# Down projection of a conv-FFN by seven quadrant products with operand sums made by accumulating DMAs in DRAM

## Chip, cores and metric

The kernel runs on one core of a Trainium2 chip. The metric is device time in microseconds (us) of one execution. TensorE, VectorE (DVE), ScalarE (ACT), GpSimd (POOL) and SyncE (SP) run side by side and wait for one another by semaphores; the last two and ScalarE also issue DMAs, which run on 16 DMA engines.

## The reference, cut to what matters

A decoder layer: a mixture of three token mixers, an output projection, and a gated FFN with a causal depthwise convolution of three taps. Sequence 1024, width 1024, FFN width 2816. The change touches the last three lines.

```python
def reference(x, norm_mix_g, w_in, ..., norm_ffn_g, w_up, conv_f_w, w_down, rel_bias, final_g):
    ...
    x = x + y @ w_out[l]
    h = rmsnorm(x, norm_ffn_g[l])
    up = causal_dwconv(h @ w_up[l], conv_f_w[l])
    gate, val = jnp.split(up, 2, axis=-1)
    x = x + (jax.nn.silu(gate) * val) @ w_down[l]
    return rmsnorm(x, final_g)
```

## The kernel before, in words

All data are float32. A product is made of three TensorE passes (`mm3`, L89 to 92): each operand is split into a rounded part `hi` and the rest `lo` (`split`, L69: a copy on ScalarE, a subtraction on VectorE or GpSimd), and hi·hi, hi·lo and lo·hi are added up in PSUM. A matmul has a 128x128 stationary and a 128x512 moving tile.

**Up projection.** `main(j)` (L973), j = 0 to 21, makes feature tile j of the gate and of the value half for 1024 tokens. It already uses seven products of quadrants instead of eight: GpSimd makes four sums of weight quadrants (L981 to 984), each operand is split into one of six slots, and TensorE runs five products of 12 matmuls (`t2`, `t3`, `t1`, `t4`, `b22`) and two more (`b11`, `b21`) for a feature tile four further on (`lead`, L945): 84 matmuls, 60 in mains 6, 13, 20 and 21, which have no lead. The weights of a main come by two DMAs on SP (L975, L976) into one of two pairs of buffers (`ur`, `xp`), the lead's by a third (L942). At the end of a main ScalarE and VectorE do the convolution (`conv3`, L967), ScalarE the SiLU (L1015), VectorE the multiplication by the value (L1016), and SP stores the 128x1024 activation tile to DRAM (`actd`, L1017). GpSimd issues no DMA in this part.

**Down projection.** For each half h of the tokens (L1079) all 22 feature tiles are run through. For tile kt, `wd_tiles` (L1045) loads 128x1024 of `w_down` and 128x512 of `actd`, splits both, and TensorE adds into eight PSUM banks (four token blocks of 128 by two halves of the output columns): 24 matmuls a tile. The operands of the first two tiles are loaded and split ahead, in the places of `b11` and `b21` (`early_tiles`, L955). The eighth bank runs behind, and for the last three tiles (`LAG`) the order is by bank, so that banks end one after the other. Then VectorE adds the residual (L1108, loaded back from `x2d`), ScalarE sums squares (L1110), and `finish` (L1061) scales by the final norm and stores the output.

The order of TensorE's work is the order in the source; that of the other engines is planned at build time from modelled durations, with `tc.issue_after` forcing some of it. Each engine, SP's and GpSimd's DMA queue too, then runs its list in order: an instruction that waits for a semaphore holds up those behind it.

## Time and profile before

| | us |
|---|---|
| median of 3 runs | 1180.95 (1178.72 to 1181.68) |
| the profiled execution | 1175.46 |
| its span, first to last instruction | 1173.7 |
| TensorE busy | 1132.8 (97%) |
| VectorE busy | 757.5 (65%) |
| GpSimd busy | 523.5 (45%) |
| ScalarE busy | 503.7 (43%) |

The profiled execution lies 5.5 us below the median of the runs. "Busy" counts overlapping matmuls once; the rate of matmuls is read from their starts. The up projection's mains run from about 525 to 924 us of the span, the down projection from 924 us to the end. A row of a timeline gives start and duration in us, the engine, the line of the kernel, the operation, what it writes and reads, and in brackets the idle time before it and what ended it.

### The profile page before, as it was taken

To read this page: it belongs to the slowest core of one execution; us is meant where nothing else is said; L and a number is where in the kernel's file an instruction comes from. 1 tells how busy PE (TensorE), PEld (TensorE's weight loads), DVE (VectorE), ACT (ScalarE), POOL (GpSimd) and SP (SyncE) were. 2 spreads that over 40 slices of the span, in tenths; PEclk is the share of its full clock that TensorE was granted. 3 is DMA by queue.
4 is the path that set the end of the run, shared out by engine and by line. 5 is a ranking of instruction groups with operands and counts; after the bars stand their busy time and mean duration, and the time that the engine had idled before them with its cause. 6 is when DMAs were issued, how large, how long until landed. Compare 5 with 4: busy or idle time off the path is not lost.

```text
span 1173.7 us, 14302 instructions
## 1 busy us (share of the span) xinstructions
PE 1132.8 (97%) x5327; PEld 939.6 (80%) x5327; DVE 757.5 (65%) x886; ACT 503.7 (43%) x802; POOL 523.5 (45%) x332
## 2 busy tenths in 40 slices
PE   9999979999989999889999999999999999999997
PEld 7888867788878888778887888888887788888886
DVE  7599965456676667794768877688778722164214
ACT  7212105255566564653444444444445432333323
POOL 4223533333333112036867877777876042334331
PEclk9999989999999999989999999999999999999999
DMA  6217312977797514313333342332423564456531
GB/s 240 72 54 222 86 54 81 261 215 168 174 323 160 111 30 151 139 53 114 95 121 95 108 139 90 126 108 91 142 91 125 170 206 156 140 184 214 180 113 72
DMA packets 58741, 160.70 MB, mean 137 GB/s; under 512 B 6168, under 2 KB 15888, under 8 KB 58672
## 3 DMA queue, kind: packets, MB, share of 16 engines
q1 hardware_dynamic: 45360, 141.37, 36.9%
q0 software_dynamic: 12160, 16.78, 7.6%
q10 hardware_dynamic: 1152, 1.64, 0.5%
q8 instruction: 42, 0.69, 0.2%
q14 instruction: 27, 0.22, 0.1%
HBM read 124.02 MB, written 32.60 MB: 133 GB/s over the span
## 4 chain that ended last, share of the span: by engine, by line
PE 86%; DVE 5%; DMA 4%; ACT 3%; issue 2%; POOL 1%; ACTq 0%; DVEq 0%; POOLq 0%; SPq 0%
PE cb L90 8%; PE cb L91 8%; PE cb L92 8%; PE d_ps L92 7%; PE d_ps L91 6%; PE d_ps L90 6%; PE ca L92 4%; PE ca L90 4%; PE ca L91 4%; PE pv_ps L585 2%; PE f_ps L90 2%; PE f_ps L92 2%; PE f_ps L91 2%; PE t_ps L554 2%; DMA w_raw<-in 1%
## 5 line engine op out<-in xcount | busy, mean ns | idle before, releaser
L72 POOL TENSOR_TENSOR w_lo<-w_raw,w_hi 128x512 fp32r<-128x512 f32 (+2 forms) x51 | 107.9, 2121 | 180.1 <-ACT w_hi L71 180.1
L970 DVE SCALAR_TENSOR_TENSOR x<-ut,pr,x 128x1024 f32<-128x1024 f32 x88 | 149.9, 1720 | 19.1 <-ACT x L968 18.3
L72 POOL TENSOR_TENSOR wd_lo<-w_raw,wd_hi 128x1024 fp32r<-128x1024 f32 x32 | 78.4, 2455 | 161.7 <-ACT wd_hi L71 149.1
L92 PE MATMUL d_ps<-wd_hi,a_lo 128*128 128x512 f32 x336 | 130.8, 389 | 1.2 <-DVE a_lo L72 1.2
L90 PE MATMUL d_ps<-wd_hi,a_hi 128*128 128x512 f32 x336 | 130.8, 389 | 0.5 <-ACT a_hi L71 0.5
L91 PE MATMUL d_ps<-wd_lo,a_hi 128*128 128x512 f32 x336 | 130.8, 389 | 0.5 <-POOL wd_lo L72 0.5
L72 DVE TENSOR_TENSOR a_lo<-a_raw,a_hi 128x512 fp32r<-128x512 f32 x42 | 41.8, 1004 | 126.7 <-ACT a_hi L71 120.7
L71 ACT CAST w_hi<-w_raw 128x512 fp32r<-128x512 f32 (+2 forms) x63 | 46.3, 747 | 134.4 <-PE v L92 23.6
L298 DVE SCALAR_TENSOR_TENSOR yc<-u,pr,yc 128x1024 f32<-128x1024 f32 x60 | 89.6, 1546 | 1.7 <-ACT yc L295 1.4
L92 PEld LDWEIGHTS d_ps<-wd_hi,a_lo 128*128 128x128 f32 x336 | 63.1, 188 | 14.4 <-DVE a_lo L72 1.5
L90 PEld LDWEIGHTS d_ps<-wd_hi,a_hi 128*128 128x128 f32 x336 | 63.1, 188 | 14.1 <-ACT a_hi L71 1.0
L91 PEld LDWEIGHTS d_ps<-wd_lo,a_hi 128*128 128x128 f32 x336 | 63.1, 188 | 14.0 <-POOL wd_lo L72 0.8
L71 ACT CAST a_hi<-a_raw 128x512 fp32r<-128x512 f32 x42 | 25.8, 621 | 107.2 <-PE d_ps L91 104.7
L968 ACT ACTIVATE x<-ut,pr 128x1024 f32<-128x1024 f32 x44 | 50.8, 1154 | 42.7 <-DVE ut L1010 29.2
L541 ACT ACTIVATE p<-p,mn 128x128 f32<-128x128 f32 (+3 forms) x64 | 49.7, 777 | 32.7 <-DVE mn L538 32.5
L71 ACT CAST wd_hi<-w_raw 128x1024 fp32r<-128x1024 f32 x42 | 43.9, 1047 | 23.3 <-DMA w_raw<-in 23.3
L1007 DVE TENSOR_TENSOR ut<-cb,yb 128x512 f32<-128x512 f32 x22 | 15.2, 690 | 57.1 <-PE cb L92 57.1
L565 DVE TENSOR_TENSOR ptl<-t_ps,pth 128x512 fp32r<-128x512 f32 x48 | 33.1, 689 | 22.7 <-ACT pth L564 22.2
L1016 DVE TENSOR_TENSOR x<-x 128x1024 f32<-128x1024 f32 x22 | 40.7, 1848 | 10.6 <-ACT x L1015 10.6
L554 PE MATMUL t_ps<-ident,p 128*128 128x128 f32 x288 | 44.7, 272 | 1.5 <-ACT p L541 1.1
L981 POOL TENSOR_TENSOR xp<-xp 128x512 f32<-128x512 f32 x11 | 20.0, 1819 | 55.1 <-DVE so_lo L72 43.7
L554 PEld LDWEIGHTS t_ps<-ident,p 128*128 128x128 f32 x288 | 35.7, 140 | 10.3 <-ACT p L541 1.5
(409 smaller groups left out, 3312.6 us busy)
## 6 DMA issues: line engine op xcount, KB each, us to landing
w_raw<-in SPq DMA_DIRECT2D x93, 512.0 KB, 3.7
xp<-in SPq DMA_DIRECT2D x26, 512.0 KB, 3.8
ur<-in SPq DMA_DIRECT2D x22, 512.0 KB, 3.5
actd<-x SPq DMA_DIRECT2D x22, 512.0 KB, 5.5
a_raw<-actd SPq DMA_DIRECT2D x42, 256.0 KB, 3.1
vd<-vt SPq DMA_DIRECT2D x8, 512.0 KB, 3.3
vv<-vd POOLq DMA_DIRECT2D x8, 512.0 KB, 5.4
g<-fs SPq DMA_DIRECT2D x8, 512.0 KB, 5.8
```

Of the source, the lines that this page charges most:

```text
L71: cp = A.copy(hi, src)
L72: lo_eng.tensor_tensor(out=lo, in0=src, in1=f(hi), op=ALU.subtract)
L90: T.matmul(ps, whi, xhi, start=start, stop=False, **kw)
L91: T.matmul(ps, whi, xlo, start=False, stop=False, **kw)
L92: T.matmul(ps, wlo, xhi, start=False, stop=stop, **kw)
L298: V.scalar_tensor_tensor(out=yc[i], in0=u[i][:, j:j + S], scalar=col("cwc", j * 2 + i), in1=yc[i], op0=ALU.mult, op1=ALU.add)
L541: mark["exp"] = A.activation(out=p[:, :n], in_=p[:, :n], func=AF.Exp, scale=-1.0, bias=mn[:, ix:ix + 1], accum_out=den[h // 2][:, dc:dc + 1])
L554: T.transpose(out=tp[:, i * P:(i + 1) * P], in_=p[:, kj * P:(kj + 1) * P], identity=ident)
L565: mark["v"] = V.tensor_tensor(out=tl[:, o:o + n], in0=tp[:, :n], in1=f(th[:, o:o + n]), op=ALU.subtract)
L968: A.activation(out=c, in_=t[:, 2:], func=AF.Copy, scale=col("cwf", 2 * 44 + m))
L970: V.scalar_tensor_tensor(out=c, in0=t[:, q:q + S], scalar=col("cwf", q * 44 + m), in1=c, op0=ALU.mult, op1=ALU.add)
L1016: V.tensor_tensor(out=cg, in0=cg, in1=cv, op=ALU.mult)
```

## The change

The down projection is written as a product of 2x2 quadrants and done by seven products P1 to P7 instead of eight. Quadrants of the activations: first or second 11 feature tiles (`HF`) by first or second 512 tokens. Quadrants of `w_down`: the same feature halves by output-column halves. The tiles of the second feature half are stored with the opposite sign (an operation of VectorE with scalar -1.0 in place of the multiplication), so that the differences that the scheme needs become sums.

The products want four sums of weight quadrants (T1 to T4) and four of activation quadrants (`s12` in both halves, `s3d`, `s4d`). All are made in DRAM while the up projection runs: for weights, SP copies a quadrant from DRAM to DRAM (`t_copy`, four chunks of three or two tiles per sum, mains 2 to 9) and GpSimd issues a DMA that adds another quadrant, or an earlier sum, into it (`t_add`, mains 4 to 12). The activation tile is stored two or three times (`store`), and GpSimd issues DMAs that add into the stored tiles (`sums`), up to three per main; the last ones come in steps 1, 4 and 8 of the down projection. The stores of the last two mains go out on ScalarE's queue.

In the down projection each product takes 11 steps. In a step `down_tiles` loads two 128x512 tiles (five buffers each), both are split by ScalarE and VectorE (none by GpSimd), and TensorE runs 12 matmuls into four banks; the products use two groups of four banks in turn, and P3 adds to the banks of P5. The order is P1, P2, P6, P7, P5, P4, P3. Four tiles instead of two are prepared ahead. At a product's end its four banks are combined with the residual tiles (`done1` to `done7`); the second half of the tokens is finished after P4, the first after P3.

```diff
-    actd = [dr.tile([P, S], F32, name=f"actd{j}") for j in range(FT)]
...
+    HF = FT // 2
+    CH = ((0, 3), (3, 6), (6, 9), (9, 11))
+    tsum = {n: [dr.tile([P, b - a, 544], F32, name=f"T{n}_{c}")[:, :, :512] for c, (a, b) in enumerate(CH)] for n in (1, 2, 3, 4)}
+    s12 = [dr.tile([P, S], F32, name=f"s12_{i}") for i in range(HF)]
+    s3d, s4d, a1d = ([dr.tile([P, 512], F32, name=f"{n}_{i}") for i in range(HF)] for n in ("s3d", "s4d", "a1d"))
+    a2d = [dr.tile([P, S], F32, name=f"a2d_{i}") for i in range(HF)]
+    def wquad(half, q, a, b):
+        return w_down[(half * HF + a) * P:(half * HF + b) * P, HS[q]]
+    def rows(x):
+        return x.rearrange("(t p) c -> p t c", p=P)
+    def t_copy(n, c):
+        half, q = {1: (0, 0), 3: (0, 1), 2: (1, 1), 4: (1, 0)}[n]
+        nc.sync.dma_start(out=tsum[n][c], in_=rows(wquad(half, q, *CH[c])))
+    def t_add(n, c):
+        src = rows(wquad(*{1: (0, 1), 3: (1, 1)}[n], *CH[c])) if n in (1, 3) else tsum[n // 2][c]
+        G.dma_start(out=tsum[n][c], in_=src, accum_op=ALU.add)
+    TCOPY = [(n, c) for c in range(4) for n in (1, 3, 2, 4)]
+    TADD = ((1, 0), (3, 0), (1, 1), (2, 0), (3, 1), (4, 0), (1, 2), (2, 1), (3, 2), (4, 1), (1, 3), (2, 2),
+            (3, 3), (4, 2), (2, 3), None, (4, 3), None)
+    def t_sums(j):
+        if j >= 2:
+            with tc.issue_after(mark["wu"].ins):
+                for x in TCOPY[2 * (j - 2):2 * (j - 1)]:
+                    t_copy(*x)
+    def sums(j):
+        if j >= 4:
+            with tc.issue_after(mark["a12"].ins):
+                for x in TADD[2 * (j - 4):2 * (j - 3)]:
+                    if x:
+                        t_add(*x)
+        i = j - 1
+        if 0 <= i < HF:
+            G.dma_start(out=s3d[i], in_=s12[i][:, HS[1]], accum_op=ALU.add)
+        for back, dst, src in ((1, lambda i: s12[i][:, HS[1]], lambda i: a2d[i][:, HS[1]]),
+                               (2, lambda i: s12[i][:, HS[0]], lambda i: s12[i][:, HS[1]]),
+                               (3, lambda i: s4d[i], lambda i: s12[i][:, HS[0]])):
+            i = j - back - HF
+            if 0 <= i < HF:
+                G.dma_start(out=dst(i), in_=src(i), accum_op=ALU.add)
+    def store(j, cg):
+        i = j % HF
+        if j < HF:
+            dst = ((s12[i], cg), (a1d[i], cg[:, HS[0]]), (s3d[i], cg[:, HS[0]]))
+        else:
+            dst = ((a2d[i], cg), (s4d[i], cg[:, HS[0]]))
+        for o, x in dst:
+            (nc.scalar if j >= FT - 2 else nc.sync).dma_start(out=o, in_=x)
+    def a_of(t, q=None):
+        return lambda i: t[i] if q is None else t[i][:, HS[q]]
+    def b_of(half, q):
+        return lambda i: wquad(half, q, i, i + 1)
+    def t_of(n):
+        return lambda i: tsum[n][i // 3][:, i % 3, :]
+    SRC = {"P1": (a_of(a1d), b_of(0, 0)), "P2": (a_of(a2d, 0), b_of(1, 0)), "P6": (a_of(s12, 0), t_of(2)),
+           "P7": (a_of(s3d), t_of(3)), "P5": (a_of(s12, 1), t_of(1)), "P4": (a_of(a2d, 1), t_of(4)),
+           "P3": (a_of(s4d), b_of(1, 1))}
...
-        b = bop[("b11", "b21")[kt]]
+        hi, lo = bop[("b11", "b21")[kt // 2]]
         raw = wp.tile([P, D], F32, name="w_raw", tag="w_raw", bufs=2)
-        nc.sync.dma_start(out=raw, in_=w_down[kt * P:(kt + 1) * P, :])
-        hi, lo = (t.rearrange("p k c -> p (k c)") for t in b)
-        split(raw, hi[:, :1024], lo[:, :1024], V)
-        ar = f(hi[:, 1536:])
-        nc.sync.dma_start(out=ar, in_=actd[kt][:, HS[0]])
-        split(ar, hi[:, 1024:1536], lo[:, 1024:1536], V)
-        return hi[:, :1024], lo[:, :1024], hi[:, 1024:1536], lo[:, 1024:1536]
+        r = []
+        for n, src in enumerate(SRC["P1"]):
+            x = raw[:, HS[n]]
+            nc.sync.dma_start(out=x, in_=src(kt))
+            k = 2 * (kt % 2) + n
+            split(x, hi[:, k, :], lo[:, k, :], V)
+            r += [hi[:, k, :], lo[:, k, :]]
+        return r
...
-        nc.sync.dma_start(out=g, in_=w_up[2 * j])
+        mark["wu"] = nc.sync.dma_start(out=g, in_=w_up[2 * j])
+        t_sums(j)
...
+            mark["a12"] = G.tensor_tensor(out=a12, in0=a12, in1=a11, op=ALU.subtract)
...
         o = operand(a12, G)
+        sums(j)
...
-        V.tensor_tensor(out=cg, in0=cg, in1=cv, op=ALU.mult)
-        nc.sync.dma_start(out=actd[j], in_=cg)
+        if j < HF:
+            V.tensor_tensor(out=cg, in0=cg, in1=cv, op=ALU.mult)
+        else:
+            V.scalar_tensor_tensor(out=cg, in0=cg, scalar=-1.0, in1=cv, op0=ALU.mult, op1=ALU.mult)
+        store(j, cg)
...
-            early[j - FT + 3] = early_tiles(j - FT + 3)
-    close(c_um, c_h2, held["xp"], c_y, c_mm)
+            for q in range(2):
+                early[2 * (j - FT + 3) + q] = early_tiles(2 * (j - FT + 3) + q)
...
+    NBUF = LAG + 2
+    x3 = [dn.tile([P, D], F32, name=f"x3_{t}") for t in range(8)]
+    for e in "ab":
+        for n, dt in (("raw", F32), ("hi", F32R), ("lo", F32R)):
+            for _ in range(NBUF):
+                dn.tile([P, 512], dt, name=f"{e}_{n}", tag=f"{e}_{n}", bufs=NBUF)
+    p1, u2, u3 = ([dn.tile([P, 512], F32, name=f"{n}_{t}") for t in range(4)] for n in ("p1", "u2", "u3"))
...
-    def wd_tiles(kt, h):
-        if h == 0 and kt in early:
-            return early[kt]
-        hs = slice(h * 512, (h + 1) * 512)
-        raw = wp.tile([P, D], F32, name="w_raw", tag="w_raw", bufs=2)
-        nc.sync.dma_start(out=raw, in_=w_down[kt * P:(kt + 1) * P, :])
-        wh = dn.tile([P, D], F32R, name="wd_hi", tag="wd_hi", bufs=NBUF)
-        wl = dn.tile([P, D], F32R, name="wd_lo", tag="wd_lo", bufs=NBUF)
-        split(raw, wh, wl, V if kt % 4 == 3 else G)
-        ar = dn.tile([P, 512], F32, name="a_raw", tag="a_raw", bufs=NBUF)
-        nc.sync.dma_start(out=ar, in_=actd[kt][:, hs])
-        ah = dn.tile([P, 512], F32R, name="a_hi", tag="a_hi", bufs=NBUF)
-        al = dn.tile([P, 512], F32R, name="a_lo", tag="a_lo", bufs=NBUF)
-        split(ar, ah, al, V)
-        return wh, wl, ah, al
+    def down_tiles(n, kt):
+        r = []
+        for e, src in zip("ab", SRC[n]):
+            raw = dn.tile([P, 512], F32, name=f"{e}_raw", tag=f"{e}_raw", bufs=NBUF)
+            mark["down"] = nc.sync.dma_start(out=raw, in_=src(kt))
+            hi = dn.tile([P, 512], F32R, name=f"{e}_hi", tag=f"{e}_hi", bufs=NBUF)
+            lo = dn.tile([P, 512], F32R, name=f"{e}_lo", tag=f"{e}_lo", bufs=NBUF)
+            split(raw, hi, lo, V)
+            r += [hi, lo]
+        return r
+    def square(t, dh):
+        q = HS[dh]
+        A.activation(out=xo[t % 2][:, q], in_=x3[t][:, q], func=AF.Square,
+                     accum_out=s3[:, 2 * t + dh:2 * t + dh + 1])
...
+            (nc.scalar if last is not None and q == HS[0] else nc.sync if t < 4 else G).dma_start(
+                out=out[t * P:(t + 1) * P, q], in_=x[:, q])
...
+    def dmm(n, y, t, kt, ops, start=True):
+        if (n, t) not in banks:
+            banks[n, t] = dps.tile([P, 512], F32, name=f"d_{y}{t}", tag=f"d_{y}{t}") if start else banks[start_of[n], t]
+        ah, al, bh, bl = ops
+        ts = slice(t * P, (t + 1) * P)
+        mm3(banks[n, t], ah[:, ts], al[:, ts], bh, bl, start and kt == 0, kt == HF - 1,
+            **({} if start else {"skip_group_check": True}))
...
+    XAT = (5, 6, 7, 8, 30, 32, 34, 36)
+    ORDER = ("P1", "P2", "P6", "P7", "P5", "P4", "P3")
+    def run(n, y, done):
+        lag = LAG if n == ORDER[-1] else 1
         tiles = {}
-
-        def dmm(b, kt):
-            if b not in ps:
-                ps[b] = dps.tile([P, 512], F32, name=f"d_ps{b}", tag=f"d_ps{b}")
-            wh, wl, ah, al = tiles[kt]
-            ts, ds = slice(b // 2 * P, (b // 2 + 1) * P), HS[b % 2]
-            mm3(ps[b], ah[:, ts], al[:, ts], wh[:, ds], wl[:, ds], kt == 0, kt == FT - 1)
-
-        for kt in range(FT - LAG):
-            tiles[kt] = wd_tiles(kt, h)
-            for b in range(7):
-                dmm(b, kt)
-            if kt == LAG - 1:
-                for q in range(kt + 1):
-                    dmm(7, q)
-            elif kt >= LAG:
-                dmm(7, kt)
-        for kt in range(FT - LAG, FT):
-            tiles[kt] = wd_tiles(kt, h)
+        for kt in range(HF):
+            step = ORDER.index(n) * HF + kt
+            if step in XAT:
+                t = XAT.index(step)
+                with tc.issue_after(mark["down"].ins):
+                    nc.sync.dma_start(out=x3[t], in_=x2d[t])
+            if step == XAT[-1]:
+                with tc.issue_after(mark["down"].ins):
+                    nc.sync.dma_start(out=gfrow, in_=grow[1:2, :].broadcast_to([P, D]))
+            if step in (1, 4, 8):
+                sums(FT + (1, 4, 8).index(step))
+            ops = tiles[kt] = early[kt] if n == "P1" and kt in early else down_tiles(n, kt)
+            if kt < HF - lag:
+                for t in range(4):
+                    dmm(n, y, t, kt, ops, n not in start_of)
         for t in range(4):
-            nc.sync.dma_start(out=x3[t], in_=x2d[4 * h + t])
-        for b in range(8):
-            for kt in range(FT - LAG, FT):
-                dmm(b, kt)
-            t, q = 4 * h + b // 2, HS[b % 2]
-            x = x3[b // 2][:, q]
-            V.tensor_tensor(out=x, in0=ps[b], in1=x, op=ALU.add)
-            o = xo[b // 2 % 2]
-            A.activation(out=o[:, q], in_=x, func=AF.Square, accum_out=s3[:, 2 * t + b % 2:2 * t + b % 2 + 1])
-            if t == 7 and b % 2 == 0:
-                G.tensor_tensor(out=o[:, q], in0=x, in1=gfrow[:, q], op=ALU.mult)
-            if b % 2:
-                finish(t, o if t == 7 else None)
-    close(c_dp, c_dn, c_h, c_w, c_pad, c_const, c_dr)
+            for kt in range(HF - lag, HF):
+                dmm(n, y, t, kt, tiles[kt], n not in start_of)
+            done(t, banks[n, t])
...
+    def done1(t, ps):
+        A.copy(p1[t], ps)
+        tt(x3[t][:, HS[0]], ps, x3[t][:, HS[0]])
+    def done2(t, ps):
+        tt(x3[t][:, HS[0]], x3[t][:, HS[0]], ps, ALU.subtract)
+        square(t, 0)
+    def done6(t, ps):
+        tt(u2[t], p1[t], ps, ALU.subtract)
+        if t == 3:
+            for q in range(4):
+                tt(x3[q][:, HS[1]], x3[q][:, HS[1]], u2[q], ALU.subtract)
+    def done7(t, ps):
+        tt(u3[t], ps, u2[t])
+        if t == 3:
+            for q in range(4):
+                for h, op in zip(HS, (ALU.subtract, ALU.add)):
+                    tt(x3[4 + q][:, h], x3[4 + q][:, h], u3[q], op)
+    def done5(t, ps):
+        tt(x3[4 + t][:, HS[1]], ps, x3[4 + t][:, HS[1]])
+        square(4 + t, 1)
+    def done4(t, ps):
+        x = x3[4 + t][:, HS[0]]
+        tt(x, x, ps, ALU.subtract)
+        square(4 + t, 0)
+        finish(4 + t, None)
+    def done3(t, ps):
+        x, o = x3[t], xo[t % 2]
+        if t == 3:
+            tt(o[:, HS[0]], x[:, HS[0]], gfrow[:, HS[0]], ALU.mult, G)
+        tt(x[:, HS[1]], x[:, HS[1]], ps, ALU.subtract)
+        square(t, 1)
+        finish(t, o if t == 3 else None)
```

## Rows read from the trace of the kernel before

**Rows 1.** The page's part 1: busy us, share of the span, instructions.

```profile
PE 1132.8 (97%) x5327; PEld 939.6 (80%) x5327; DVE 757.5 (65%) x886; ACT 503.7 (43%) x802; POOL 523.5 (45%) x332
```

**Rows 2.** The page's part 4: shares of the chain that ended last.

```profile
PE 86%; DVE 5%; DMA 4%; ACT 3%; issue 2%; POOL 1%; ACTq 0%; DVEq 0%; POOLq 0%; SPq 0%
```

**Rows 3.** Windows: us, busy us by engine (count), TensorE clock, DMA share, GB/s.

```profile
601.00:710.00 109.00, 108.27 (x478) 89.34 (x477) 83.72 (x74) 48.43 (x70) 82.97 (x50) 1.00 0.34 111
...
924.03:937.28 13.25, 11.03 (x47) 8.37 (x45) 9.83 (x9) 7.67 (x10) 2.38 (x1) 1.00 0.74 258
937.28:1150.00 212.72, 212.72 (x940) 176.13 (x939) 63.78 (x74) 68.63 (x98) 76.01 (x31) 1.00 0.52 168
...
1166.62:1173.70 7.08, 0.00 (x1) 0.00 (x0) 1.96 (x6) 1.65 (x4) 1.21 (x1) 0.83 0.38 148
```

**Rows 4.** TensorE in the down projection, timeline: start, us, line, operation.

```profile
924.03 0.39 PE L90 MATMUL d_ps<-b11h 128*128 128x512 f32 x1
...
933.33 0.39 PE L92 MATMUL d_ps<-b21h,b21l 128*128 128x512 f32 x1
...
937.28 0.39 PE L90 MATMUL d_ps<-wd_hi,a_hi 128*128 128x512 f32 x1
...
1166.23 0.39 PE L92 MATMUL d_ps<-wd_hi,a_lo 128*128 128x512 f32 x1
```

**Rows 5.** TensorE in the up projection, first product of two mains, timeline.

```profile
653.63 0.39 PE L90 MATMUL cb<-t2h,w_hi 128*128 128x512 f32 x1
...
672.67 0.39 PE L90 MATMUL cb<-t2h,w_hi 128*128 128x512 f32 x1
```

**Rows 6.** ScalarE where the up projection ends, timeline.

```profile
929.22 1.06 ACT L1015 ACTIVATE x<-x 128x1024 f32<-128x1024 f32 x1 [2.67 <-DVE x L970]
...
930.30 1.28 ACT L107 ACT_TABLE_LOAD   x1
...
931.71 1.98 ACT L71 CAST wd_hi<-w_raw 128x1024 fp32r<-128x1024 f32 x2
```

**Rows 7.** Splits of 512 columns: VectorE 950 to 1140 us, ScalarE (page, part 5).

```profile
L72 DVE TENSOR_TENSOR a_lo<-a_raw,a_hi x36: 679/693/2880, 949.5 to 1139.9; 128x512 fp32r<-128x512 f32 x36
...
L71 ACT CAST a_hi<-a_raw 128x512 fp32r<-128x512 f32 x42 | 25.8, 621 | 107.2 <-PE d_ps L91 104.7
```

**Rows 8.** VectorE and the last store around the last matmul, timeline.

```profile
1165.42 1.28 DVE L1073 SCALAR_TENSOR_TENSOR x<-x,s,gfrow 128x1024 f32<-128x1024 f32 x1
...
1166.66 0.69 DVE L1108 TENSOR_TENSOR x<-d_ps,x 128x512 f32<-128x512 f32 x1
...
1168.20 0.16 DVE L1065 TENSOR_TENSOR s<-s 128x1 f32<-128x1 f32 x1 [0.85 <-ACT xo L1110]
...
1169.01 0.75 DVE L1073 SCALAR_TENSOR_TENSOR x<-x,s,gfrow 128x512 f32<-128x512 f32 x1
...
1169.83 0.37 ACTq L1074 DMA_DIRECT2D out_dram<-x  x1
```

**Rows 9.** DMA queues: packets, MB, share; whole run, then 601 to 710 us.

```profile
q0 software_dynamic: 12160, 16.78, 7.6%
...
q1 hardware_dynamic: 3312, 12.06, 33.9%
```

**Rows 10.** SP queue and GpSimd preparing the main of 672.67 us, timeline.

```profile
643.63 0.33 SPq L975 DMA_DIRECT2D ur<-in  x1
...
647.14 1.29 POOL L981 TENSOR_TENSOR s1t<-ur 128x512 f32<-128x512 f32 x1 [5.23 <-DMA ur<-in]
```

**Rows 11.** DMAs issued by GpSimd: ns min/median/max of the issue.

```profile
L394 POOL DMA_DIRECT2D sm<-qk x12: 557/567/580, 248.1 to 378.1; - x12
...
L398 POOL DMA_DIRECT2D vv<-vd x8: 889/935/1076, 111.8 to 395.4; - x8
```

**Rows 12.** Waits of GpSimd, 525 to 905 us: us in total, times, longest.

```profile
POOL w_lo L72 <- ACT w_hi L71: 33.7, 16, 4.1
...
POOL xp L982 <- DMA xp<-in: 14.5, 8, 3.5
```

More of the change, by code (lines that the diff above doesn't have):

```diff
@@ L983, in main @@
             G.tensor_tensor(out=a11, in0=s1, in1=a11, op=ALU.subtract)
-            G.tensor_tensor(out=a12, in0=a12, in1=a11, op=ALU.subtract)
+            mark["a12"] = G.tensor_tensor(out=a12, in0=a12, in1=a11, op=ALU.subtract)
         ug, uv = ut
@@ L1031, in body @@
         if j in (FT - 3, FT - 2):
-            early[j - FT + 3] = early_tiles(j - FT + 3)
-    close(c_um, c_h2, held["xp"], c_y, c_mm)
+            for q in range(2):
+                early[2 * (j - FT + 3) + q] = early_tiles(2 * (j - FT + 3) + q)
+    close(c_um, c_h2, held["xp"], c_y, c_w, c_mm)
     c_dn, dn = pool("dn", "left")
@@ L1038, in body @@
     LAG = 3
-    NBUF = LAG + 1
+    NBUF = LAG + 2
[5 more added lines that the diff above has]
+    p1, u2, u3 = ([dn.tile([P, 512], F32, name=f"{n}_{t}") for t in range(4)] for n in ("p1", "u2", "u3"))
     gfrow = dn.tile([P, D], F32, name="gfrow")
     xo = [dn.tile([P, D], F32, name="xo", tag="xo", bufs=2) for _ in range(2)]
-    x3 = [dn.tile([P, D], F32, name=f"x3_{t}") for t in range(4)]
-    def wd_tiles(kt, h):
-        if h == 0 and kt in early:
-            return early[kt]
-        hs = slice(h * 512, (h + 1) * 512)
-        raw = wp.tile([P, D], F32, name="w_raw", tag="w_raw", bufs=2)
-        nc.sync.dma_start(out=raw, in_=w_down[kt * P:(kt + 1) * P, :])
-        wh = dn.tile([P, D], F32R, name="wd_hi", tag="wd_hi", bufs=NBUF)
-        wl = dn.tile([P, D], F32R, name="wd_lo", tag="wd_lo", bufs=NBUF)
-        split(raw, wh, wl, V if kt % 4 == 3 else G)
-        ar = dn.tile([P, 512], F32, name="a_raw", tag="a_raw", bufs=NBUF)
-        nc.sync.dma_start(out=ar, in_=actd[kt][:, hs])
-        ah = dn.tile([P, 512], F32R, name="a_hi", tag="a_hi", bufs=NBUF)
-        al = dn.tile([P, 512], F32R, name="a_lo", tag="a_lo", bufs=NBUF)
-        split(ar, ah, al, V)
-        return wh, wl, ah, al
+    def down_tiles(n, kt):
[12 more added lines that the diff above has]
+                     accum_out=s3[:, 2 * t + dh:2 * t + dh + 1])
     def finish(t, last):
-        x, c = x3[t % 4], slice(t, t + 1)
+        x, c = x3[t], slice(t, t + 1)
         r = s3[:, 16:][:, c]
@@ L1068, in finish @@
         V.reciprocal(out=r, in_=r)
-        for q in HS if last else (slice(0, D),):
-            if last and q == HS[0]:
+        for q in HS if last is not None else (slice(0, D),):
+            if last is not None and q == HS[0]:
                 A.activation(out=x[:, q], in_=last[:, q], func=AF.Copy, scale=r)
@@ L1073, in finish @@
                 V.scalar_tensor_tensor(out=x[:, q], in0=x[:, q], scalar=r, in1=gfrow[:, q], op0=ALU.mult, op1=ALU.mult)
-            (nc.scalar if last and q == HS[0] else nc.sync).dma_start(out=out[t * P:(t + 1) * P, q], in_=x[:, q])
+            (nc.scalar if last is not None and q == HS[0] else nc.sync if t < 4 else G).dma_start(
+                out=out[t * P:(t + 1) * P, q], in_=x[:, q])
     table(AF.Sqrt, "silu")
     s3 = const.tile([P, 24], F32, name="s3")
-    nc.scalar.dma_start(out=gfrow, in_=grow[1:2, :].broadcast_to([P, D]))
@@ L1115, in body @@
-    close(c_dp, c_dn, c_h, c_w, c_pad, c_const, c_dr)
+    banks = {}
+    def dmm(n, y, t, kt, ops, start=True):
[5 more added lines that the diff above has]
+            **({} if start else {"skip_group_check": True}))
+    start_of = {"P3": "P5"}
@@ new lines, in tt @@
+    def tt(o, a, b, op=ALU.add, eng=V):
+        eng.tensor_tensor(out=o, in0=a, in1=b, op=op)
+    def done1(t, ps):
[15 more added lines that the diff above has]
+                    tt(x3[4 + q][:, h], x3[4 + q][:, h], u3[q], op)
@@ L1116, in body @@
+    run("P1", "x", done1)
+    run("P2", "y", done2)
+    run("P6", "x", done6)
+    run("P7", "y", done7)
+    run("P5", "x", done5)
+    run("P4", "y", done4)
+    run("P3", "x", done3)
+    close(c_dp, c_dn, c_h, c_pad, c_const, c_dr)
     ms.__exit__(None, None, None)
```

2 lines of the change are left out of this document (removed).

## Prediction, made before the changed kernel had run

> **What bounds the kernel now.** I read the profile from the whole to the stage. The page's first part has TensorE busy for 97% of the span [rows 1], and the chain that ended last runs through PE for 86% [rows 2]: look there for which engine time can be bought from. The windows say in which stage. From 601 to 710 us, mains 4 to 9 of the up projection, TensorE is busy 108.3 of 109 us, GpSimd 83.0, VectorE 83.7, the DMA engines 34% at 111 GB/s; from 937 to 1150, in the down projection, it is busy all the time while VectorE has 30%, ScalarE 32%, DMA 52% [rows 3]. The granted clock is 1.00 in both, the 2.4 GHz level. So in both stages the end is set by the number of matmuls, and what other engines do is free as long as operands come in time.
>
> The price of a matmul comes from starts, not from the 0.39 us that a record shows, since matmuls overlap. From 937.28 to 1166.23 us lie 1010 intervals (the 46th to the 1056th matmul of the stage): 0.2267 us each. The first 42 take 0.2268 [rows 4]. In the up projection one main of 84 matmuls takes 19.04 us, 0.2267 again [rows 5].
>
> **Removed: matmuls.** Now: 2 halves x 22 tiles x 8 banks x 3 = 1056. After: 7 products x 11 tiles x 4 token blocks x 3 = 924, same shapes, the same alternation of stationary tiles. 132 x 0.2267 = **-29.9 us**, wholly on the path.
>
> **Start of the down projection.** Now the 43rd matmul should follow 933.33 at once, but 937.28 is reached 3.0 us late: four matmuls in 3.95 us [rows 4]. ScalarE is the cause: its queue holds the last convolution, then the table load, and casts only from 931.71 [rows 6]. The change keeps that order, but 48 instead of 42 matmuls use early tiles (to 924.03 + 10.9 = 934.9 us), and the first new tile wants two casts of 0.62 us and two subtractions of 0.69 [rows 6, 7], ready about 934.0. The two stores of the last main move into ScalarE's queue and wait there for the final multiplication, with those casts behind them; at 0.37 us an issue [rows 8] they use the margin up. Gain 0 to 3.0; I take **-2.5**. The early tiles have 4096 columns to split instead of 3072: 1.4 us more on VectorE beside the last mains, which have little cover; 0 to 1.4, taken at **+0.7**.
>
> **Steps of the down projection.** A step is now 12 matmuls, 2.72 us. It wants two casts (1.24 us), two subtractions on VectorE (1.38; today's stretched ones reach 2.88 because GpSimd works beside them, which it no longer does) [rows 7], and 524 KB, which at 326 GB/s (below) is 1.6 us. Five buffers for each operand give 13.6 us of cover to the load. A product's end adds up to 12 operations of 0.69 us in a burst [rows 8], which five prepared steps outlast. So **0**, at most 3 us. The loads of the second residual half lie beside matmuls.
>
> **The end.** Now each token block has two banks before its closing operations; after, one bank of 9 matmuls, 2.04 us. VectorE needs 0.69 + 3 x 0.16 + 1.28 = 2.45 us per block [rows 8], so the last block starts 3 x 0.4 = 1.2 us behind, and two round trips to ScalarE sit in each chain. 0 to 4, taken at **+2.5**. From the last matmul to the end it is 7.1 us now [rows 3].
>
> **DMAs added beside the up projection.** Rates: mains 4 to 9 move 12.06 MB in 33.9% of 109 us, 326 GB/s of DMA-engine time; GpSimd's queue moved 16.78 MB in 7.6% of 1173.7, 188 GB/s [rows 9]. No row shows a transfer from DRAM to DRAM, nor an accumulating one. Call the price of an accumulated byte k times that of a plain one: k = 1 at least (it moves no less), 1.73 if like GpSimd's queue. Mains 2 to 12 last 204 us. Present traffic takes 34%, 69 us [rows 3]; 11.5 MB of copies 35; 5.2 MB of additional stores 16: together 120. Accumulated: 11.5 MB of weight sums and 2.9 MB of activation sums, 44k us. k = 1 gives 164 of 204, k = 1.73 gives 196. In the peak, mains 4 to 9, it is 72 + 33k of 109, 20 late at 1.73. So the engines are nearly full, and late at the peak, but nothing on the path wants these sums before the third product, 60 us into the next stage. What may be late is a load of up weights. A main's load goes out at 643.63 and its first product runs at 672.67 [rows 5, 10]: 29.0 us, of which load (3.5 us to 647.14), four pre-additions and a subtraction at 1.66 (82.97 us over 50) and a cast need 12.4. Spare 16 us. I take **0**, bounds 0 and 14.
>
> The Trainium skill, page "Collectives: The Full Stack", section "The bandwidth ceiling: the fold count and why AG ≠ RS ≠ AR", speaks against this change: an add in the DMA path needs two source reads, so it runs at half the rate of a copy, k = 2. By it the sum would be the first rival's 1165 instead of 1152; with k = 1 it stays 1152. No row of this case shows which.
>
> **GpSimd.** It issues the accumulating DMAs: two weight sums and one activation sum in a main, later three activation sums. An issue of 64 rows took 0.57 us, one of 1024 runs 0.94 [rows 11]; with 384 rows 0.69, so 1.95 us per main against (109 - 83) / 5.7 = 4.6 us of idle. Behind a waiting issue stand the pre-additions of the next main but one and the subtractions of operands, and TensorE waits for those. GpSimd's idle time is waiting for ScalarE's paced casts and for loads, 33.7 and 14.5 us in its longest lines [rows 12], which can take this in. Most sums wait for something a main older; only the first activation sum waits for stores of the main before. **0**. SP gets up to four more issues per main at 0.33 us [rows 10], hidden in its waits. The negation replaces one VectorE operation by another of the same size: 0.
>
> **Sum.** -29.9 - 2.5 + 0.7 + 2.5 = -29.2 us. The profiled execution took 1175.46 us around a span of 1173.7 and would become 1146. The three runs shown have a median 5.5 us above it, so 1180.95 - 29.2 = **1152**. With the bounds of start, steps and end: 1147 to 1159.
>
> **Rivals.** *Loads late in the up projection.* At k = 2 an accumulated byte occupies the engines twice; mains 4 to 9 then want 138 of 109 us, 29 late, 13 beyond the spare 16: 1165. At k = 2.5, or if GpSimd's waits on unfinished copies exceed its remaining 2.6 us per main, up to 25: 1157 to 1177. For it: 72 + 33k exceeds 109 at any k above 1.1. Against: two queues share the engines, and GpSimd's may fall behind unpunished.
> *DMA-bound up projection, slower.* Place: mains 2 to 12. Loss beyond the spare: 120 + 44k - 204 - 16; it exceeds the gain of 29 from k about 2.9, the point from which it decides against the change. At k = 3.5 the loss is 54: 1206. For it: an unseen kind of transfer, all of it on the engines that feed TensorE. Against: GpSimd's queue needs only 1.73 times the plain price with its 512-byte runs, here 2 KB.
> *The down projection becomes load-bound.* Its traffic rises from 168 to 193 GB/s [rows 3], all in 2 KB rows. If these ran at half rate, a step would want 3.2 us instead of 2.72: 66 x 0.5 = 33 us, which cancels the gain: the change then removes matmuls but no time, 1178 to 1185. Against: the start of the stage reached 258 GB/s.
>
> **Chances.** Forecast 0.60 (1147 to 1159); late loads 0.19 (to 1177); load-bound 0.05; slower 0.12; below 1147 0.04. The range 1147 to 1177 holds the first two. Within 0.3% of 1180.95 is 3.5 us, about what a measurement can tell from no change: faster 0.83, same 0.05, slower 0.12.
>
> **What would show it.** After: matmul starts of 0.227 us in both stages, 924 in the down projection; first down matmul still near 924 us of the span; TensorE's end about 209 us later; no wait of a matmul for a cast after the early tiles; DMA share of 0.8 to 1.0 in mains 4 to 9. Wrong if the first down matmul moves past 930 (the sums cost the up projection), if mains 4 to 12 are longer than 19.04 us with waits on loads or on GpSimd, or if steps exceed 2.72 us. The step most likely wrong is the price of the accumulating DMAs.

## The result and the profile after

The changed kernel takes **1228.93 us** (median of 4 runs, 1219.22 to 1234.62) against 1179.84 for the kernel before: 1.041 times its time, 95% interval 1.034 to 1.048. Forecast were 1152 and a gain; 1228.93 lies above the range, and the sign is wrong. The profiled execution has a span of 1227.4 us.

The page's part 1 (busy us, share of the span, instructions) and the shares of its part 4, which answer to [rows 1, 2]:

```profile
PE 1129.7 (92%) x5195; PEld 928.7 (76%) x5195; DVE 864.3 (70%) x1008; ACT 521.0 (42%) x872; POOL 468.4 (38%) x364
...
PE 63%; DVE 11%; DMA 10%; issue 6%; POOL 6%; ACT 3%; SPq 0%; POOLq 0%; ACTq 0%; DVEq 0%
```

There are 132 matmuls fewer, as meant, but PE's share of the chain falls from 86% to 63%, and VectorE, DMAs and GpSimd take its place. To find the stage, take one product that every kernel runs in the same mains; the pair of times in its row is its first and its last start. Its row before, its row after, and then the first and the last matmul of the down projection after:

```profile
L90 PE MATMUL cb<-t3h,w_hi x64: 389/389/389, 527.5 to 915.2; 128*128 128x512 f32 x64
```

```profile
L90 PE MATMUL cb<-t3h,w_hi x64: 389/389/389, 531.0 to 996.3; 128*128 128x512 f32 x64
```

```profile
1005.16 0.39 PE L90 MATMUL d_x<-b11h 128*128 128x512 f32 x1
...
1217.86 0.39 PE L92 MATMUL d_x<-b_hi,a_lo 128*128 128x512 f32 x1
```

The up projection grew from 387.7 to 465.3 us, **+77.6**. The down projection went from 242.2 [rows 4] to 212.7 us, **-29.5**. From the start of the last matmul to the end of the span it is 9.5 us instead of 7.5 (1166.23 to 1173.7; the 7.1 of [rows 3] count from that matmul's end). The product above also starts 3.5 us later; over all kernels of this document whose source is the same up to there, that start lies between 524.7 and 533.5. The miss lies in the up projection, where the forecast had put 0. The windows of the changed kernel, columns as in [rows 3]:

```profile
601.00:710.00 109.00, 94.99 (x394) 76.37 (x394) 81.55 (x59) 39.37 (x57) 74.90 (x57) 0.94 0.94 248
...
767.00:860.00 93.00, 83.04 (x356) 67.23 (x354) 81.18 (x58) 36.13 (x52) 61.11 (x47) 0.97 0.56 139
860.00:950.00 90.00, 77.75 (x307) 62.78 (x308) 60.15 (x43) 30.26 (x43) 53.76 (x44) 0.89 0.55 132
```

There are two different losses. From 601 to 710 us TensorE starts 394 matmuls instead of 478 [rows 3] with the DMA engines 94% busy. From 767 on the DMA engines are at 55%, and still 307 matmuls start in 90 us where 0.2267 us each would give 397. GpSimd's timeline from 850 to 862 us, and the first three rows of TensorE's behind it, show why (in brackets: idle time before, and what ended it):

```profile
850.76 0.81 POOL L1004 DMA_DIRECT2D s<-a2d  x1
851.33 1.73 POOL L72 TENSOR_TENSOR so_lo<-w_raw,so_hi 128x512 fp32r<-128x512 f32 x1
855.60 0.83 POOL L1004 DMA_DIRECT2D s<-s  x1 [2.55 <-DMA s<-a2d]
860.24 0.82 POOL L1004 DMA_DIRECT2D s4d<-s  x1 [3.80 <-DMA s<-s]
860.78 1.56 POOL L72 TENSOR_TENSOR so_lo<-w_raw,so_hi 128x512 fp32r<-128x512 f32 x1
...
862.40 0.80 PE L92 MATMUL ca<-b11h,so_lo 128*128 128x512 f32 x1 [8.47 <-POOL so_lo L72]
862.99 0.63 PE L90 MATMUL ca<-b11h,so_hi 128*128 128x512 f32 x1
863.41 0.63 PE L91 MATMUL ca<-b11l,so_hi 128*128 128x512 f32 x1
```

The three later additions of one tile stand back to back. Each reads what the one before writes, so the second is issued 4.8 us and the third 9.5 us after the first; the subtraction of an operand stands behind them, and TensorE waits 8.47 us for it. The first matmul then takes 0.80 us instead of 0.39 and the next ones start 0.43 us apart instead of 0.23; the granted clock from 862.4 to 865.4 us is 0.50, the 1.2 GHz level. So a wait costs more than its length: from 860 to 950 us TensorE is busy 77.75 us with 307 matmuls, which at 0.2267 would be 69.6. Of the 20.4 us lost there 12.3 are idle time and, by this estimate, 8.2 are matmuls at a lower clock (0.89 over the window).

The source puts these additions one, two and three mains after the tile's own, but the order on GpSimd is planned at build time, and the plan put all three of a tile together. The rows leave buffer numbers out; that the tile is one and the same is seen at the start, where the first addition of each kind is issued at 803.34, 807.91 and 812.12 us, where by the source a whole main lies between them.

Waits from 525 to 1000 us (total, times, longest), GpSimd's, then TensorE's; the first two answer to [rows 12]:

```profile
POOL xp L1057 <- DMA xp<-in: 26.8, 7, 5.1
POOL w_lo L72 <- ACT w_hi L71: 26.4, 9, 4.6
POOL ur L1057 <- DMA ur<-in: 24.5, 8, 4.8
POOL s4d L1004 <- DMA s<-s: 22.6, 8, 4.1
POOL s L1004 <- DMA s<-a2d: 13.3, 6, 3.9
...
PE ca L92 <- POOL w_lo L72: 15.4, 5, 4.7
PE cb L90 <- DVE ut L1073: 15.2, 5, 5.8
PE ca L92 <- POOL so_lo L72: 11.9, 3, 8.5
```

GpSimd waits for loads (26.8 + 24.5 us; 14.5 and 14.1 before) and for its own additions. TensorE waits for GpSimd (15.4 + 11.9) and for VectorE (15.2, where it was 0.8 before).

### The profile page after: what moved, and what is told of

Read it like the earlier page. It is cut to its first block, busy times and chain, and to the rows that moved or that the text cites. A ratio compares the mean times of both kernels' runs of the same rounds, so it can differ in the third digit from the quotient of the medians.

```text
span 1227.4 us, 14660 instructions
## 1 busy us (share of the span) xinstructions
PE 1129.7 (92%) x5195; PEld 928.7 (76%) x5195; DVE 864.3 (70%) x1008; ACT 521.0 (42%) x872; POOL 468.4 (38%) x364
## 4 chain that ended last, share of the span: by engine, by line
PE 63%; DVE 11%; DMA 10%; issue 6%; POOL 6%; ACT 3%; SPq 0%; POOLq 0%; ACTq 0%; DVEq 0%
DVE x L1044 5%; PE cb L90 4%; PE cb L91 4%; PE cb L92 4%; PE ca L92 3%; PE ca L90 3%; PE ca L91 3%; PE d_x L91 3%; PE d_x L92 3%; PE d_x L90 3%; PE d_y L90 2%; PE d_y L91 2%; PE d_y L92 2%; PE pv_ps L585 2%; PE f_ps L90 2%
## 5 line engine op out<-in xcount | busy, mean ns | idle before, releaser
L1044 DVE SCALAR_TENSOR_TENSOR x<-ut,pr,x 128x1024 f32<-128x1024 f32 x88 | 170.8, 1956 | 24.5 <-ACT x L1042 23.7
L71 ACT CAST w_hi<-w_raw 128x512 fp32r<-128x512 f32 (+2 forms) x63 | 46.3, 747 | 134.4 <-PE v L92 23.6
L90 PE MATMUL d_x<-b_hi,a_hi 128*128 128x512 f32 x160 | 62.5, 391 | 1.8 <-ACT b_hi L71 1.7
L91 PE MATMUL d_x<-b_lo,a_hi 128*128 128x512 f32 x160 | 62.5, 391 | 0.4 <-DVE b_lo L72 0.4
L92 PE MATMUL d_x<-b_hi,a_lo 128*128 128x512 f32 x160 | 62.3, 389 | 0.0
L1091 ACT ACTIVATE x<-x 128x1024 f32<-128x1024 f32 x22 | 23.3, 1061 | 79.1 <-DVE x L1044 79.1
L90 PE MATMUL d_y<-b_hi,a_hi 128*128 128x512 f32 x132 | 51.3, 389 | 0.0
L91 PE MATMUL d_y<-b_lo,a_hi 128*128 128x512 f32 x132 | 51.3, 389 | 0.0
L92 PE MATMUL d_y<-b_hi,a_lo 128*128 128x512 f32 x132 | 51.3, 389 | 0.0
L72 DVE TENSOR_TENSOR b_lo<-b_raw,b_hi 128x512 fp32r<-128x512 f32 x73 | 50.0, 685 | 1.6 <-ACT b_hi L71 1.6
L71 ACT CAST b_hi<-b_raw 128x512 fp32r<-128x512 f32 x73 | 45.0, 617 | 2.0 <-DMA b_raw<-in 1.1
L538 DVE CUSTOM_DVE_ANT_0 p<-l_ps,g 128x640 f32<-128x640 f32 (+5 forms) x34 | 33.8, 994 | 14.0 <-PE l_ps L532 13.4
```

Source lines behind the costliest of these rows:

```text
L71: cp = A.copy(hi, src)
L72: lo_eng.tensor_tensor(out=lo, in0=src, in1=f(hi), op=ALU.subtract)
L90: T.matmul(ps, whi, xhi, start=start, stop=False, **kw)
L91: T.matmul(ps, whi, xlo, start=False, stop=False, **kw)
L92: T.matmul(ps, wlo, xhi, start=False, stop=stop, **kw)
L538: V.tensor_tensor_reduce(out=p[:, :n], in0=ps[:, :n], in1=gq, op0=ALU.add, op1=ALU.min, scale=1.0, scalar=3e38, accum_out=mn[:, ix:ix + 1])
```

## The experiments

Two explanations stood against each other: the additions hold up GpSimd's queue (issues and waits), or their bytes fill the DMA engines and delay the loads of up weights. Each ratio is to the kernel before on the same chip, whose median was 1178.73 to 1180.46 in these groups of runs; differences between rows are therefore good to some 2 us. "Up" is the stretch of the product above, first to last start:

| kernel | us | ratio, 95% | up, us |
|---|---|---|---|
| no sums | 1148.49 | 0.965 to 0.980 | 387.6 |
| activation sums only | 1194.93 | 1.005 to 1.020 | 428.0 |
| the same, unchained copies | 1161.09 | 0.982 to 0.987 | 398.2 |
| issues only | 1164.10 | 0.985 to 0.990 | 403.7 |
| weight sums only | 1169.75 | 0.988 to 0.993 | 409.8 |
| the same, plain copies | 1157.74 | 0.978 to 0.987 | 397.1 |
| the same, copies on SP | 1155.25 | 0.977 to 0.982 | 397.3 |
| spread by a main | 1207.43 | 1.012 to 1.033 | 442.9 |
| all sums spread | 1193.36 | 1.008 to 1.013 | 427.3 |
| weight sums early | 1205.26 | 1.018 to 1.028 | 424.6 |
| all spread, weight sums early | 1180.83 | 0.999 to 1.004 | 400.3 |
| paced | 1170.67 | 0.991 to 0.996 | 403.8 |

**No sums.** The copies and additions are gone; the products read unsummed quadrants.

```diff
-                for x in TCOPY[2 * (j - 2):2 * (j - 1)]:
-                    t_copy(*x)
...
-                        t_add(*x)
...
-            G.dma_start(out=s3d[i], in_=s12[i][:, HS[1]], accum_op=ALU.add)
...
-                G.dma_start(out=dst(i), in_=src(i), accum_op=ALU.add)
```

> Left out: all copies and additions of weight quadrants (the products read a plain quadrant instead) and all additions of activation tiles; the stores, the seven products and their operand loads stay. Theory A (the loss of some 80 us sits in the up projection and comes from the sums alone, through two mechanisms: DMA engines full while the weight sums are made, mains 2 to 12, and GpSimd standing in its queue for one activation sum to land before it issues the next of the same tile, mains 12 to 21): about 1151 us, mains of 19.0 us throughout. Theory B (the sums' traffic on the DMA engines alone is the cause): also about 1151. Theory C (the additional stores and VectorE's work are a large part of it): over 1175.

1148.49. First and last matmul of the down projection, in this run's timeline:

```profile
928.19 0.39 PE L90 MATMUL d_x<-b11h 128*128 128x512 f32 x1
...
1138.10 0.39 PE L92 MATMUL d_x<-b_hi,a_lo 128*128 128x512 f32 x1
```

The down projection takes 209.9 us, 32.3 less than before, and the end 9.5 (its span is 1147.6). The up stretch is 387.6 us against 387.7, so the additional stores and VectorE's negation cost nothing that can be told. All terms of the prediction but those of the DMAs and of GpSimd are thereby measured together: -30.8 us (1148.49 against 1179.31 on its chip) where -29.2 was summed. The sums cost 1228.93 - 1148.49 = **80.4 us**.

**One kind of sum alone.** Only the weights' lines taken out, then only the activations'.

> Left out: the copies and additions of weight quadrants; the products read a plain quadrant. The activation sums stay as they are. Theory A: mains 2 to 11 take 19.0 us, mains 12 to 21 stay as long as in the changed kernel, some 42 us lost there: about 1193 us, with GpSimd waiting for landed sums as long as before. Theory B: DMA engines are half free in mains 12 to 21, so hardly any loss is left: about 1155 us.

> Left out: all additions of activation tiles (the plain stored tiles are read). The weight sums stay as they are. Theory A: the loss of mains 2 to 12, some 35 us, stays and the later mains take 19.0 us: about 1186 us. Theory B: most of the loss stays, since the weight sums are half of the accumulated bytes and all of the copies, and it lies where the DMA engines are full: about 1186 us as well; this run tells the sizes apart, not the theories.

1194.93 and 1169.75: +46.4 and +21.3 over no sums, so the two together cost 12.7 more than the sum of each alone. The 1186 that both theories expected of the second run was 16 too high. Windows with the activation sums alone, then with the weight sums alone:

```profile
767.00:860.00 93.00, 81.27 (x331) 64.62 (x330) 71.62 (x53) 33.55 (x48) 55.80 (x45) 0.93 0.55 130
860.00:950.00 90.00, 76.39 (x308) 61.01 (x307) 78.78 (x56) 34.27 (x52) 55.44 (x45) 0.93 0.54 132
```

```profile
601.00:710.00 109.00, 95.88 (x398) 76.74 (x397) 87.10 (x62) 38.74 (x57) 73.22 (x53) 0.95 0.92 256
...
767.00:860.00 93.00, 92.43 (x408) 76.25 (x407) 74.88 (x64) 42.27 (x59) 77.14 (x45) 1.00 0.37 127
```

With the activation sums alone the DMA engines are at 55% from 767 to 950 us, and matmuls are lost all the same; with the weight sums alone nearly all of the loss lies at 601 to 767 us, where the DMA share reaches 0.92.

**Are they issues, bytes or waits?** In place of each activation addition GpSimd issues a plain copy of 256 KB from the weights into a buffer of its own, behind its main's own work (weight sums left out):

```diff
-                G.dma_start(out=dst(i), in_=src(i), accum_op=ALU.add)
+                with tc.issue_after(mark["a12"].ins):
+                    G.dma_start(out=fresh(), in_=wquad(0, 0, i, i + 1))
```

> The weight sums are left out, as in the run with the activation sums only (1194.93), and in the place of each activation addition GpSimd issues, in the same main, a plain copy of 256 KB from the weights into a buffer of its own, so that none waits for another (the sums are left out). It parts that run's 46 us into issues with their bytes, and waits. Theory A (the waits of one addition for the one before are the larger part; issues cost some 0.3 us each by the run with tiny copies): 44 issues, most of them in the up projection, give 1158 to 1170. Theory B (issues and bytes are most of it): 1180 to 1195.

1161.09: of the 46.4 us only 12.6 are left. The other 33.8 us go with three things that this run takes away at once: the waits of one addition for the one before, the accumulating, and the planner's freedom to place them. That the waits are the larger part is argued, not shown: the engines have room there, and from 525 to 965 us TensorE's waits for GpSimd are 20.6 us with the activation sums alone (9.0 + 8.4, below, and 3.2) against 1.8 with the copies.

```profile
PE ca L92 <- POOL w_lo L72: 9.0, 3, 3.1
PE ca L92 <- POOL so_lo L72: 8.4, 2, 6.1
```

In the next run a copy of 128 rows of 32 bytes stands for each of the 60 additions:

> All sums are left out (the products read unsummed parts, as in the kernel without sums, 1148.5); in the place of each addition GpSimd issues a copy of 128 rows of 32 bytes, in its own main, waiting for nothing. It measures what the issues alone cost, without bytes and without waits. Theory A (VectorE's longest operations, 1.75 us each without sums and 2.05 to 2.4 us with them, are stretched by GpSimd's issuing): the multiply-adds of the residual stream on VectorE grow to 2.0 us or more between 601 and 860 us, and the time to 1153 to 1165. Theory B (the stretch comes from the bytes or the waits): they stay at 1.75 and the time at 1147 to 1151.

1164.10. The issues alone, with hardly any bytes and no waits for one another, cost 15.6 us. GpSimd's timeline there:

```profile
797.64 1.55 POOL L1011 DMA_DIRECT2D tiny<-in  x3
```

An issue takes 0.52 us, 60 of them 31 us, and half of that arrives on the path. (An accumulating issue has a longer record, 0.81 us above, but GpSimd's next operation starts 0.57 us after it.) GpSimd's idle time was no reserve. In this run TensorE's waits for GpSimd are 0.9 us from 525 to 940 us; the larger wait is for VectorE's `ut`, 8.3 us, where it was 1.6 with no sums. So part of the cost comes by way of VectorE. Its multiply-adds (L1044 after, L970 before), from 767 to 860 us: before, after, and with tiny copies (busy us, mean ns, idle before):

```profile
L970 DVE SCALAR_TENSOR_TENSOR x<-ut,pr,x 128x1024 f32<-128x1024 f32 x22 | 38.9, 1790 | 2.7 <-ACT x L968 2.6
```

```profile
L1044 DVE SCALAR_TENSOR_TENSOR x<-ut,pr,x 128x1024 f32<-128x1024 f32 x19 | 45.7, 2428 | 3.8 <-ACT x L1042 3.7
```

```profile
L1051 DVE SCALAR_TENSOR_TENSOR x<-ut,pr,x 128x1024 f32<-128x1024 f32 x20 | 36.6, 1847 | 4.0 <-ACT x L1049 3.9
```

Two rows of VectorE in the changed kernel, with GpSimd's rows between them, tell why these lengthen. One multiply-add takes 4.34 us; GpSimd runs two operations on SBUF tiles inside it, from 803.91 to 806.70, 2.8 of the 3.1 us that it takes longer. The same operation at 814.73 runs while GpSimd stands idle (from 814.2 to 819.8) and takes 1.27. From 525 to 1000 us the 84 multiply-adds take 1.27 to 6.80 us (median 1.71), while the 21 operations of L1086, which have one operand in PSUM (`cb`), all take 0.68 to 0.69:

```profile
803.45 4.34 DVE L1044 SCALAR_TENSOR_TENSOR x<-ut,pr,x 128x1024 f32<-128x1024 f32 x1 [1.22 <-ACT x L1042]
...
803.91 1.55 POOL L1059 TENSOR_TENSOR ur<-ur 128x512 f32<-128x512 f32 x1
805.17 1.53 POOL L72 TENSOR_TENSOR w_lo<-xp,w_hi 128x512 fp32r<-128x512 f32 x1
...
814.73 1.27 DVE L1044 SCALAR_TENSOR_TENSOR x<-ut,pr,x 128x1024 f32<-128x1024 f32 x1
```

The Trainium skill, page "SBUF — State Buffer", section "Who interferes with whom", says that a VectorE instruction with two SBUF inputs contends with a GpSimd instruction that reads SBUF, and one with at most one such input, outside VectorE's two-port modes, does not; these rows agree. So an addition that bunches GpSimd's operations can also lengthen VectorE's. What this lengthening costs by itself is not shown: in the paced kernel below the multiply-adds take 2241 ns in the same window, and it loses only 10 matmuls of 412 there. The time of the run with tiny copies fell into the range of its first theory, but the multiply-adds did not quite reach the 2.0 us that this theory wanted from 601 to 860 us: 1974 ns to 710, 1847 ns after 767.

**The price of an accumulated byte.** The weight sums' additions made plain copies, on GpSimd's queue, then on SP's (sums left out):

```diff
-        G.dma_start(out=tsum[n][c], in_=src, accum_op=ALU.add)
+        G.dma_start(out=tsum[n][c], in_=src)
```

> Only the weight sums' transfers, and the additions among them made plain copies of the same shapes on GpSimd's queue (the sums are left out, and those of the activations too). With the additions it took 1169.75. Theory A (the 21 us come from the accumulated bytes costing about twice a plain byte in mains 2 to 12): the loss falls by half or more, 1149 to 1159. Theory B (they come from the SP copies ahead of the loads and from the issues on GpSimd, alike for a copy and an addition): 1167 to 1171.

> Only the weight sums' transfers, all as plain copies, and those in the additions' place issued on SP's queue and not on GpSimd's (sums left out, those of the activations too). On GpSimd's queue the same copies took 1157.74, no transfers 1148.49. Theory A (the 9 us are GpSimd's issues, which stretch VectorE): 1147 to 1151. Theory B (they are the bytes on the DMA engines, 23 MB more in mains 2 to 12): 1155 to 1161.

1157.74 and 1155.25: the 21.3 us fall to 9.3 and 6.8. The queue makes no difference that can be told (up stretch 397.1 and 397.3); the bytes and the copies ahead of loads cost 7 to 9 us, and that they are accumulated some 12 to 14 (the three runs behind 1157.74 reach from 1156.99 to 1165.08). GpSimd's queue (packets, MB, share of the 16 engines' span) with no sums, with the activation additions, and with the unchained copies:

```profile
q0 software_dynamic: 12736, 18.88, 7.9%
```

```profile
q0 software_dynamic: 19072, 30.42, 14.3%
```

```profile
q0 software_dynamic: 16256, 30.42, 10.9%
```

With spans of 1147.6, 1193.3 and 1159.3 us that is 91, 171 and 126 us: the same 11.54 MB take 80 us accumulated and 36 copied, 144 and 323 GB/s of engine time, **k = 2.2** (the copies read the weights, the additions stored tiles). For the weight sums (13.6% of 1169.3 against 11.1% of 1154.9) it is 68 against 37 us, k = 1.8.

**Spreading the additions.** First the last two of a tile come two mains later, all three held behind their main's own work (`issue_after(mark["a12"].ins)`, as above):

```diff
-                               (2, lambda i: s12[i][:, HS[0]], lambda i: s12[i][:, HS[1]]),
-                               (3, lambda i: s4d[i], lambda i: s12[i][:, HS[0]])):
+                               (4, lambda i: s12[i][:, HS[0]], lambda i: s12[i][:, HS[1]]),
+                               (5, lambda i: s4d[i], lambda i: s12[i][:, HS[0]])):
```

> All sums stay, the same DMAs and bytes. The second and third addition of an activation tile are put four and five mains after its making and are held behind that main's weight preparation in GpSimd's queue, so that each finds the one before it landed. Theory A: GpSimd's waits for landed activation sums (some 65 us in the changed kernel) nearly vanish and the loss of mains 12 to 21 with them: about 1187 us. Theory B: the same traffic, so the same time: about 1229 us.

1207.43, halfway between its two theories, 1187 and 1229. From 767 to 860 us 388 matmuls run instead of 356; mains 4 to 12 stay as bad as they were (393 from 601 to 710). Next all four additions of a tile, at distances of four, four, five and six mains; then the change's own order with the weight sums made ahead of the up projection; then both:

> All of the sums are kept; the first addition of a tile comes four mains after its stores, the three later ones four, five and six mains after the second half's, and each is held behind the GpSimd work of its own main; what is left over goes into steps 1, 3, 5, 7, 9 and 11 of the down projection. Theory A (most of the loss that is not the weight sums' is GpSimd standing in its queue while the addition before lands): the waits of GpSimd for s3d, s and s4d fall from 75 us in sum to under 10, TensorE is at its full pace from 767 us on, and what stays is the loss of the weight sums alone, 1169.75 measured with those alone: 1168 to 1180. Theory B (the loss is the traffic itself, wherever the additions stand): nothing changes against the spreading by one main each, 1200 to 1215.

> The activation sums as the change has them, the weight sums ahead of the up projection (projections and attention). Theory A (the activation additions alone cost 46 us, the weight sums 21 and the two together 13 more because they share mains 4 to 12): about the 1194.93 measured with the activation sums alone, 1192 to 1200. Theory B (moving the weight sums only moves their cost): 1210 to 1230.

> As the spreading over four to six mains, and beside that the copies and additions of the weights' quadrant sums are made ahead of the up projection: some in the projections, the rest one every six chunks in attention, where the copies no longer stand between the loads of the up projection's weights. Theory A (the weight sums cost 21 us only because they fall on mains 2 to 12, which load 4 MB each two mains and have few bytes to spare): nothing of their cost is left, 1146 to 1156, faster than the kernel before (1179) by 2 to 3%. Theory B (an accumulated byte costs the same wherever it is moved, through GpSimd's and SP's queues): 1168 to 1190.

1193.36, 1205.26 and 1180.83: none reached its first theory. The additions spread still cost 1193.36 - 1169.75 = 23.6 us beside the weight sums, half of the 46.4; the unchained copies account for 12.6 of these, and the waits that stay (9.8 us for `s4d`, 4.0 for `s`, from 525 to 970 us) may account for some of the rest. Against the change itself the spreading, with the same additions and bytes, saves 35.6 us (1228.93 - 1193.36): where they stand decides that much. The early weight sums cost where they were moved to: the product above starts at 545.2 us instead of 531.8 in the run without sums. And what was left for the down projection was pulled into the last mains: in the last of these three, GpSimd issues nine additions from 917.9 to 934.0 us, and from 920 to 940 TensorE starts 55 matmuls where the full rate gives 88.

**Paced.** Weight sums one copy and one addition per main from main 0; two or fewer activation additions per main; the last 21 behind a one-column copy on GpSimd that reads the tile of a down step, so that the plan can't pull them forward:

```diff
+            if 4 <= step < 4 + len(DADD):
+                mark["poolq"] = G.tensor_copy(out=pace, in_=f(ops[3][:, 0:1]))
+                late_add(*DADD[step - 4])
```

> All sums kept, GpSimd's additions thinned out: the weight sums' copies and additions one at each main from main 0 on (four copies in the projections); the additions to s3 in mains 4 to 14; twelve of the other activation additions in mains 15 to 21, one or two at a main; the remaining 21 in steps 4 to 24 of the down projection, each held behind a one-column GpSimd copy that reads that step's own tile, so that they can't be pulled forward into the last mains. Theory A (what is left of the loss in the two spread kernels, 33 to 45 us over the kernel without sums, is additions that meet each other or latency-bound steps: 13 us in the projections and attention, 13 in the last two mains, 8 at the start of the down projection): most of it goes, 1158 to 1170, faster than the kernel before. Theory B (each addition costs about the same wherever it stands, some 0.5 us): 1175 to 1190.

**1170.67** (1169.05 to 1172.65), 0.9935 of the kernel before, interval 0.991 to 0.996: with the same sums it beats both kernels, by 8 and 58 us, and lies just above the 1170 that its first theory allowed. Its windows:

```profile
601.00:710.00 109.00, 104.11 (x443) 83.56 (x442) 83.47 (x71) 45.30 (x64) 76.06 (x54) 0.98 0.78 217
...
767.00:860.00 93.00, 92.24 (x402) 75.09 (x402) 81.94 (x62) 40.23 (x58) 77.13 (x49) 1.00 0.57 152
```

22 us over no sums remain: 16 in the up projection, 7 in the down projection, whose first loads now run beside the additions (DMA share 1.08 from 966 to 990 us).

## Why the prediction was wrong

**Matmuls, -29.9: right.** In the changed kernel 212.7 us hold 923 intervals of 0.2267, 209.2, and 3.5 us of stalls.

**Start of the down projection, -2.5: right without the sums, not with them.** The 3.0 us stall is gone in the run with no sums (209.9 us). No run parts out the +0.7 for the early tiles beside the last mains. In the changed kernel 3.5 us of stalls stand in its place, 1.7 of them one wait for a cast while the last additions share the engines with the loads.

**Steps 0, end +2.5: right.** Without the sums, stalls in the down projection come to 0.7 us in all; the end grew by 2.1 (9.5 against 7.5).

**DMAs beside the up projection, 0: mis-sized.** The mechanism was named (engines over-full in mains 4 to 9, loads late), and its bounds 0 to 14 were too low: the weight sums alone cost 21.3. The accumulated byte cost 1.8 to 2.2 plain ones, where 1.73 was taken from other transfers of the same queue; and the "spare 16 us" of a load was counted as if none were waited for, while GpSimd waited 53.8 us for loads of up weights before (525 to 1000 us, four rows, 14.5 of them in [rows 12]). Here the rule of the Trainium skill's page "Collectives: The Full Stack" (section "The bandwidth ceiling: the fold count and why AG ≠ RS ≠ AR"), two reads for an add and so half the rate of a copy, k = 2, lies between the two measured figures, and the row I chose below both. The page says it of a collective between cores; that the second read is the reason here too is not shown. By it the forecast would have been 1165, which the changed kernel misses by 64.

**GpSimd, 0: the step that failed.** "Most sums wait for something a main older" took the order of the source for the order of the queue. The plan set the three later additions of a tile side by side, and each wait stopped everything behind it: 33.8 us in the activation sums alone went when the copies stood in their place, the larger part of it, by the argument above, for these waits. And "1.95 us per main against 4.6 us of idle" took idle time for a reserve: the issues alone cost 15.6 us. I take the reason to be that its idle moments are waits for casts and loads, that the work behind each wait is wanted at once, and that what is packed closer stretches VectorE's operations (TensorE's wait for VectorE grew from 1.6 to 8.3 us there); these shares were not measured apart. A rival had named the waits on unfinished copies, with at most 25 us for all late loads.

**The slower rival** had the right sign for the wrong reason: it asked for k of 2.9, and the loss came at 1.8 to 2.2.

The 80.4 us as far as runs part them: 12.6 activation additions as issues and plain bytes, 33.8 their waits, accumulating and placing together, 9.3 weight sums as issues and plain bytes, 12.0 that these accumulate, 12.7 that both run in the same kernel. That last figure is only a remainder; no run took it apart. Nor was the planner's own estimate of an addition looked at, so why it set them together stays open.

## What to carry to other kernels

A DMA that an engine issues costs that engine its issue and, in order, every wait that it carries: before moving a chain of dependent DMAs to a queue that also computes, ask in which order they will stand there and what stands behind them, and hold each link to a later step. Idle time of an engine is a reserve only if its waits don't end just before work that others need. Count a transfer that accumulates at about two plain bytes (1.8 to 2.2 here), and spread such transfers over all stages with room, not over the nearest.

## What the runs showed that was not expected

Accumulating from DRAM to DRAM ran at 144 to 169 GB/s of engine time where the same copies ran at 307 to 323. A VectorE operation with two SBUF operands took 1.27 us while GpSimd stood idle and 4.34 with two GpSimd operations inside it; one with a PSUM operand kept its 0.68. A wait of TensorE cost more than its length, since the matmuls behind it ran at a lower clock (0.50 for 3 us after a wait of 8.47).
